# Attention order by a planner: when the sums, the squares, the value transposes and the output weights are given out

## The chip, the cores and the metric

The kernel runs on one core of a Trainium2 chip. The metric is device time in microseconds of one execution. Its engines work side by side: TensorE (PE in the profile, with PEld for its weight loads), VectorE (DVE), ScalarE (ACT), GpSimd (POOL) and SyncE (SP), which issues DMAs.

## The reference

One layer of a decoder trunk on 1024 rows of width 1024. What matters here, cut from the reference:

```python
h = _rmsnorm(x, g_mix);  proj = h @ w_in               # Q, K, V of both groups
# 8 stick-breaking heads of 64, in blocks of 128 queries over the causal prefix
log_survive = lax.cumsum(log_keep, axis=3, reverse=True) - log_keep
weights = jnp.where(strict, jnp.exp(log_beta + log_survive), 0.0)
o_sb = weights @ v                                      # per block
# 4 differential heads: two softmaxes (ALiBi), value width 128
attn = probs[:, :, 0] - lam * probs[:, :, 1];  o_df = attn @ v
o_sb = _rmsnorm(o_sb, g_sb_out);  o_df = _rmsnorm(o_df, g_df_out) * (1.0 - lambda_init)
x = x + jnp.concatenate([o_sb, o_df], axis=-1) @ w_out
# then RMSNorm, a router (1 of 4 groups, 2 of its 4 experts), 16 SwiGLU experts,
# a sigmoid-gated per-layer input and a last RMSNorm
```

The squares of each group's output must be summed over all its heads before a row can be normalised; only then can the output projection of a block of 128 rows begin.

## The kernel before

Float32 operands are split in a high part and a rest (names ending in h or hi, and l or lo), and a product is three matmuls. The stages: input norm and the first pair's projections to about 50 us; the attention, pair by pair, to about 530 us; the output projection in eight blocks of 128 rows (b0 to b7), with the router of the block before; then the experts, the per-layer input and the last norm.

There are 8 pairs of attention work, 0 to 3 stick-breaking and 4 to 7 differential. While a pair's attention runs, TensorE also computes this pair's V (two halves, v0 and v1) and the next pair's K and Q. Pair 7 has no next pair: it carries its own V only, and the weights of the output projection are loaded and split beside it (`out_weights`, L1048 ff: ScalarE writes `woh`, L1061, VectorE the rest `wol`, L1062).

A unit is one head and 256 query rows. Its steps: scores (L361/L362), on VectorE, ScalarE and GpSimd the weights (differential: L432 score and maximum, L439 and L448 exponentials, L450 combination), transposes of the weights (L378, `turn`) with a split to `wth`/`wtl` (L54/L55), value products (L488 to L491) into the one bank `pv`, a copy to `ot` (L499; three buffers), and `finish_o`: the DMA of `ot` to memory, its square on ScalarE (L791) and, for the differential pairs and the last stick-breaking one, the sums over rows as small matmuls with ones (L800) into a score bank.

The order on TensorE is written out by a planner, the class `Mix`, which keeps a model of the time of each engine. It holds five queues: scores S, transposes T, values V, finishes F and projection items P. In each turn `ready_x` says when the head of queue x could go; the first of V, T, S, F that is ready goes, unless the projections lag. `on(eng, ready, dur, first)` models work on another engine; `first` is work emitted under high priority. Only TensorE's order is written by hand (`manual_schedule`); VectorE's and ScalarE's is set by the tile scheduler, with precedence for what stands under `high_priority`. V's projection is drained through `vt` (one buffer, L278 on ScalarE), transposed on TensorE (L283, the `turns` of the diff) and split.

`phase_attention` runs the planner until no projection item is left and at most three finishes are (`len(mix.F) <= 3`); what is left then is mixed with blocks b0, b1 and b2 by `run_items`. A block b of the output projection begins with `normed`: the scale of its rows (`rs_*` on VectorE from `ss`), two kinds of transposes (L1134, L1140), scalings (L1136, L1141), a split, then 16 times three matmuls (L1162 to L1164). `tail` and `routes` of the block before stand among them (L1194, L1210, L1327, L1343).

Of the kernel before, what the change touches and what calls it, by code (L numbers as in the profile page):

```python
# [11 lines left out]
AF = mybir.ActivationFunctionType  # L12
# [231 lines left out]
def evac_k(k, P):  # L244
    nc = k.nc

    def f(s0, s1, ps):
        s = slice(s0, s1)
        for i, (a, b) in enumerate(ROWS2):
            oa, ob = ROWS2[1 - i]  # L250
            nc.scalar.activation(P.K[i][a:b, s], ps[a:b], AF.Copy)
            nc.vector.tensor_tensor(P.K[i][oa:ob, s], ps[a:b], P.K[i][a:b, s].bitcast(FT), OP.subtract)
    return f
# [61 lines left out]
def alloc_pair(k, P, pool):  # L315
    P.K = [pool.tile([128, S], FR, name=f"K{i}") for i in range(2)]
    P.Qh = [pool.tile([128, S], FR, name=f"Qh{i}") for i in range(2)]
    P.Ql = [pool.tile([128, S], FR, name=f"Ql{i}") for i in range(2)]
    P.V = [pool.tile([128, NB, 128], FR, name=f"V{i}") for i in range(2)]


def weights_item(k, P, i, eng=None):
    def f():
        P.W[i] = load_w(k, P.cols[i], eng)
    return (0.0, f)


def value_projection(k, P):

    g = group_items(k, lambda: P.W[2], HALVES, evac_v(k, P))  # L330
    turn = (0.45, lambda: P.turns.pop(0)())
    return g[:4] + [turn], g[4:] + [turn]
# [124 lines left out]
def units_of(k, P):  # L457

    units, OT = [], {}
    for pr in range(NB // 2):  # L460
        for h in range(1 if P.df else 2):
            u = Ctx()
            u.P, u.pr, u.h, u.rows, u.score, u.W = P, pr, h, [], [], {}
            for ii in range(2):
                i = 2 * pr + ii
                u.score.append((i, df_row_items(k, P, i, u.rows) if P.df else sb_row_items(k, P, h, i, u.rows)))
            u.turn = lambda g, u=u: turn_rows(k, u.pr, u.rows, g, u.W)
            u.value = lambda g, u=u: value(k, u, g, OT)
            u.last = P.df or h == 1
            u.finish = lambda u=u: finish_o(k, OT[u.pr], u.P, u.pr)  # L470
            units.append(u)
    return units
# [62 lines left out]
class Mix:  # L535
# [3 lines left out]
    def __init__(self, k, wt):  # L539
        self.k, self.wt = k, wt  # L540
        self.pe, self.at = 0.0, {"act": 0.0, "dve": 0.0, "pool": 0.0}
        self.S, self.T, self.V, self.F, self.P = [], [], [], [], []
        self.zfree, self.tpfree, self.pvfree, self.mmfree = [0.0] * 3, [0.0] * 2, [0.0], [0.0] * 2
        self.done, self.tot = {}, {}
        self.nT = self.nV = 0
        self.emit = lambda c, f: f()

    def on(self, eng, ready, dur, first=False):

        start = max(self.at[eng], ready)  # L550
        self.at[eng] = start + dur
        return (min(start, ready + 0.7) if first else start) + dur

    def add_pair(self, P, p, units, proj):
        main = 0.0
# [65 lines left out]
    def ready_v(self):  # L621
        u, g = self.V[0]
        if g not in u.wready or not u.values(g):
            return None
        return max(u.wready[g], self.pvfree[0] if g == 0 else 0.0)

    def do_v(self):
# [11 lines left out]

    def ready_f(self):  # L640
        u = self.F[0]
        return u.out + 1.0 if u.vals == u.pr + 1 else None

    def do_f(self):
        u = self.F.pop(0)
        self.emit(0.11, u.finish)
        self.on("act", self.pe, 0.4)
        self.pe += 0.3 if u.P.df or u.P.ch == 3 else 0.0

    def ready_p(self):  # L650
        p, kind, c, f, ok = self.P[0]
# [4 lines left out]
    def do_p(self):  # L656
        p, kind, c, f, ok = self.P.pop(0)
        f()
        self.pe += c
        self.done["p", p] += c  # L660
        if kind == "weights":
            self.on("dve", self.on("act", self.pe + 4.0, 1.1), 1.25)
        if kind == "last":
            a = self.on("act", self.pe, 1.2, True)
            self.mmfree = self.mmfree[1:] + [self.on("dve", a, 1.3, True)]
# [25 lines left out]
def run_pairs(k, Ps, qk, n, last):  # L691


    mix = Mix(k, 3)
    us = [units_of(k, P) for P in Ps[:n + 1]]
    every = [u for x in us for u in x]
    state = {"kq": 0, "v": {}}

    def proj(items, p, ok=None, end=None):
        out = []  # L700
        per = NC // 2
        for x, (c, f) in enumerate(items):
            kind = "last" if c > 1 and x % (per + 1 if end is None else per) == per - 1 else "mid"
            out.append([kind, c * 1.05, f, ok if x == 0 else None])
        return out

    for p in range(n + 1):
        P, Q = Ps[p], Ps[min(p + 1, n)]
        v0, v1 = value_projection(k, P)

        def group(items, ok, then):
            out = []
            for x, (c, f) in enumerate(items):
                kind = "first" if x == 0 else "last" if x == 3 else "mid"
                if x == len(items) - 1:
                    g = f
                    f = lambda g=g: (g(), then())
                out.append((kind, c * 1.05, f, ok if x == 0 else None))
            return out

        def counted(p, x):
            return lambda: state["v"].__setitem__((p, x), True)

        def alloc(Q=Q, p=p):
            alloc_pair(k, Q, qk[p % 2])

        def free(p=p):
            return p == 0 or all(u.vals == u.pr + 1 for u in us[p - 1])

        def load(Q, i):  # L730
            return ("weights", 0.0, weights_item(k, Q, i)[1], None)


        w0 = load(Q, 0)
        w1 = load(Q, 1)
        w2 = load(Q, 2)
        turns = [("mid", 0.45, v[4][1], None) for v in (v0, v1)]
        for x in range(2):
            kd, c, f, ok = turns[x]
            turns[x] = (kd, c, lambda f=f, p=p, x=x: (f(), state["v"].__setitem__((p, x), True)), ok)  # L740
        for u in us[p]:
            u.values = lambda g, p=p: (p, g // 2) in state["v"]
        if p == n:
            items = group(v0[:4], None, nothing) + [turns[0]] + [("mid", 0.0, f, None) for f in last[0]]
            items += group(v1[:4], None, nothing) + [turns[1]] + [("mid", 0.0, f, None) for f in last[1]]
            mix.add_pair(P, p, us[p], items)
            break
        K = group_items(k, lambda Q=Q: Q.W[0], HALVES, evac_k(k, Q))
        QQ = group_items(k, lambda Q=Q: Q.W[1], HALVES, evac_q(k, Q, Q.qscale))
        nothing_ = lambda: None  # L750
        kq = ("mid", 0.0, lambda p=p: state.__setitem__("kq", p + 1), None)
        items = [w0] + group(v0[:4], None, nothing_) + [turns[0], w1] + group(v1[:4], None, nothing_)
        items += [("mid", 0.0, alloc, free)]
        g = group(K[:4], None, nothing_)
        items += g[:1] + [turns[1]] + g[1:] + group(K[4:], None, nothing_) + [w2]
        items += group(QQ[:4], None, nothing_) + group(QQ[4:], None, nothing_) + [kq]
        for u in us[p]:
            u.values = lambda g, p=p: (p, g // 2) in state["v"]
        mix.add_pair(P, p, us[p], items)
    for x, u in enumerate(every):  # L760
        before = every[x - 2] if x >= 2 else None
        u.allowed = lambda u=u, before=before: state["kq"] >= u.p and (before is None or before.turns == before.pr + 1)
    return mix
# [18 lines left out]
def finish_o(k, ot, P, pr):  # L782
    nc = k.nc
    q = slice(pr * 256, (pr + 1) * 256)
    nc.sync.dma_start(k.oT_d[P.ch][:, q], ot)
    sums = k.sums[pr // 2][:, pr % 2 * 256:pr % 2 * 256 + 256]
    if P.df or P.ch:
        sq = k.wk.tile([128, 256], FT, name="sq", bufs=2)
    else:
        sq = sums  # L790
    nc.scalar.activation(sq, ot, AF.Square)  # L791
    if not P.df:
        if P.ch:
            nc.gpsimd.tensor_tensor(sums, sums, sq, OP.add)
        if P.ch < 3:
            return
        sq = sums
    ps = bank_z(k, P.df)
    for i in range(2):
        nc.tensor.matmul(ps[:, i:i + 1], sq[:, i * 128:(i + 1) * 128], k.ones, start=True, stop=True)  # L800
    nc.scalar.activation(k.ss[:, 2 * pr:2 * pr + 2, max(P.ch - 3, 0)], ps[:, 0:2], AF.Copy,
                         scale=1.0 if P.df else 0.25)
# [1201 lines left out]
```

## Time and profile before

| what | value |
|---|---|
| median of 3 runs | 1231.78 us (1230.64 to 1232.29) |
| the profiled execution | 1227.81 us |
| its span, first to last instruction | 1226.0 us |
| mean granted clock of TensorE | 0.979 |
| busy PE / DVE / ACT / POOL | 1145.5 / 923.1 / 723.0 / 207.5 us |

The span is the profiled execution less 1.8 us; that execution lies 4.0 us under the median. A window below gives the busy time of each engine in a stretch; a wait is idle time of an engine and what ended it; a timeline gives the start of an instruction, its duration, and in brackets its idle time before.

### The profile page before, as it was taken

The page shows a single profiled execution, that of the slowest core. Times are in us where ns is not written, and L with a number is a line of the kernel's source. Part 1 is how long each engine was busy: PE and PEld are TensorE (multiplying, and loading weights), DVE is VectorE, ACT ScalarE, POOL GpSimd, SP SyncE. Part 2 cuts the span into 40 slices and gives each one's busy share as a digit, 9 for nine tenths or more (in the row PEclk, how much of TensorE's full clock was granted, in tenths as well). Part 3 has the DMA queues.
Part 4 walks back from the last instruction along what each step waited for, and adds up shares of the span by engine and source line. Part 5 has one row for each costly group of instructions (what it writes and reads, how often), then busy time and mean ns, then how long its engine had stood idle before and what let it go on. Part 6 is the DMA issues. An engine that isn't in the chain of part 4 may idle for free. (4 is left out here: it accounts for less than half of the span.)

```text
span 1226.0 us, 22814 instructions
## 1 busy us (share of the span) xinstructions
PE 1145.5 (93%) x8181; PEld 826.5 (67%) x8181; DVE 923.1 (75%) x2144; ACT 723.0 (59%) x1408; POOL 207.5 (17%) x298
## 2 busy tenths in 40 slices
PE   5999999999999999889789899999999999997996
PEld 4766656665666666646444498898998989883443
DVE  7677786766766767769888777777888878765875
ACT  6476766766756576735332365666777767663432
POOL 0133333333200000002331101111112212110000
PEclk9999999999999999879899999999999999999999
DMA  6212021120222121532674878998998999937611
GB/s 208 67 30 74 30 69 32 44 60 27 57 61 65 40 65 53 171 90 102 217 234 148 298 250 262 282 352 265 316 313 283 337 280 325 304 125 298 250 71 52
DMA packets 211756, 202.54 MB, mean 165 GB/s; under 512 B 12697, under 2 KB 182681, under 8 KB 211642
## 3 DMA queue, kind: packets, MB, share of 16 engines
q1 hardware_dynamic: 205688, 180.22, 46.9%
q0 software_dynamic: 5808, 20.58, 4.5%
q8 instruction: 65, 1.06, 0.3%
q14 instruction: 49, 0.40, 0.1%
q10 hardware_dynamic: 146, 0.27, 0.1%
HBM read 163.03 MB, written 29.62 MB: 157 GB/s over the span
## 5 line engine op out<-in xcount | busy, mean ns | idle before, releaser
L228 PE MATMUL mm<-hT,whi 128*128 128x512 f32 (+1 forms) x416 | 210.9, 508 | 2.6 <-DVE rs_v L66 1.4
L229 PE MATMUL mm<-hT,whi 128*128 128x512 bf16 (+1 forms) x416 | 157.0, 377 | 4.1 <-DVE hT L184 4.1
L230 PE MATMUL mm<-hT,wlo 128*128 128x512 bf16 (+1 forms) x416 | 155.7, 374 | 0.0
L1611 PE MATMUL gu<-xh,mhiu 128*128 128x128 f32 (+4 forms) x512 | 155.1, 314 | 0.0
L1611 PE MATMUL gu<-xh,mhig 128*128 128x128 f32 (+4 forms) x512 | 153.9, 308 | 0.0
L1613 PE MATMUL gu<-xbl,mhig 128*128 128x128 bf16 (+4 forms) x512 | 124.6, 243 | 2.6 <-DVE xbl L1524 2.6
L1613 PE MATMUL gu<-xbl,mhiu 128*128 128x128 bf16 (+4 forms) x512 | 124.4, 243 | 0.0
L1614 PE MATMUL gu<-xh,mblg 128*128 128x128 bf16 (+4 forms) x512 | 119.6, 234 | 0.0
L1614 PE MATMUL gu<-xh,mblu 128*128 128x128 bf16 (+4 forms) x512 | 119.3, 233 | 0.0
L55 DVE TENSOR_TENSOR mdl<-mrawd,mdh 128x1024 bf16<-128x1024 f32 x63 | 77.0, 1222 | 44.6 <-ACT mdh L54 39.9
L54 ACT ACTIVATE wth<-tp 128x512 fp32r<-128x512 f32 (+2 forms) x168 | 70.2, 446 | 63.0 <-PE tp L378 41.0
L55 DVE TENSOR_TENSOR wtl<-tp,wth 128x512 fp32r<-128x512 f32 (+2 forms) x168 | 79.2, 493 | 36.7 <-ACT wth L54 35.3
L409 POOL TENSOR_TENSOR row<-row,keep 128x127 f32<-128x127 f32 (+3 forms) x64 | 77.9, 1218 | 143.5 <-DVE keep L408 88.4
L228 PEld LDWEIGHTS mm<-hT,whi 128*128 128x128 f32 x416 | 80.2, 193 | 30.9 <-ACT hT L183 2.0
L55 DVE TENSOR_TENSOR mblg<-mrawg,mhig 128x1024 bf16<-128x1024 f32 x62 | 75.8, 1223 | 29.8 <-ACT mhig L54 29.7
L54 ACT ACTIVATE mdh<-mrawd 128x1024 fp32r<-128x1024 f32 x64 | 67.6, 1056 | 51.8 <-PE ya L1643 47.6
L1611 PEld LDWEIGHTS gu<-xh,mhig 128*128 128x128 f32 x512 | 97.6, 191 | 0.7 <-ACT xh L1523 0.3
L229 PEld LDWEIGHTS <-whi 128*128 128x128 bf16 x416 | 40.7, 98 | 85.0 <-issue 78.6
L1611 PEld LDWEIGHTS gu<-xh,mhiu 128*128 128x128 f32 x512 | 96.7, 189 | 0.0
L408 DVE TENSOR_TENSOR_SCAN keep<-keep,zx 128x128 f32<-128x128 f32 (+3 forms) x64 | 85.4, 1346 | 14.1 <-ACT keep L404 13.4
L46 POOL DMA_INDIRECT y_d<-yo,put x27 | 44.6, 1651 | 290.0 <-ACT yo L1661 185.8
L54 ACT ACTIVATE mhig<-mrawg 128x1024 fp32r<-128x1024 f32 x64 | 67.4, 1053 | 19.2 <-PE gu L1614 11.9
(348 smaller groups left out, 3346.6 us busy)
## 6 DMA issues: line engine op xcount, KB each, us to landing
mrawg<-in_w_expert_gate_dram SPq DMA_DIRECT2D x64, 512.0 KB, 5.8
mrawu<-in_w_expert_up_dram SPq DMA_DIRECT2D x64, 512.0 KB, 6.4
mrawd<-in_w_expert_down_dram SPq DMA_DIRECT2D x64, 512.0 KB, 4.3
wraw<-in_w_in_dram SPq DMA_DIRECT2D x24, 512.0 KB, 3.9
yg<-y_d SPq DMA_DIRECT2D x16, 512.0 KB, 5.7
xt<-in_x_dram SPq DMA_DIRECT2D x8, 512.0 KB, 6.6
oT_d<-ot SPq DMA_DIRECT2D x32, 128.0 KB, 2.1
wraw<-in_w_out_dram SPq DMA_DIRECT2D x8, 512.0 KB, 3.6
```

Of the source, the lines that this page charges most:

```text
L46: i = k.nc.gpsimd.indirect_dma_start(out=out, out_offset=bass.IndirectOffsetOnAxis(ap=idx, axis=0), in_=src, in_offset=None)
L54: nc.scalar.activation(hi, src, AF.Copy)
L55: (eng or nc.vector).tensor_tensor(lo, src, hi.bitcast(FT), OP.subtract)
L228: nc.tensor.matmul(ps, hi[:, c, :], hT[:, c % 4, :], start=(c == 0), stop=False)
L229: nc.tensor.matmul(ps, wv[:, c, :], k.hT[half][2][:, c, o:o + n], start=False, stop=False)
L230: nc.tensor.matmul(ps, lo[:, c, :], hv[:, c % 4, :], start=False, stop=(c == NC - 1))
L408: nc.vector.tensor_tensor_scan(a, a, k.zeros.to_broadcast([128, n]), 1.0, op0=OP.mult, op1=OP.add)
L409: nc.gpsimd.tensor_tensor(beta[:, :n - 1], beta[:, :n - 1], keep[:, 1:n], OP.mult)
L1611: nc.tensor.matmul(ps[:, x], hi[:, c], xh[:, c], start=(c == 0), stop=False)
L1613: nc.tensor.matmul(ps[:, x], hv[:, c], xl[:, c], start=False, stop=False)
L1614: nc.tensor.matmul(ps[:, x], bl[:, c], xv[:, c], start=False, stop=(c == NC - 1))
```

## The change

`Mix.on` models boosted work as starting when it is ready, or at the end of the run that then stands on the engine (before: at most 0.7 us late). A unit's last value item is held back while two of the first three finishes have their values but are not given out. A finish is given out 2.0 us after its output (before 1.0), once a score bank is modelled free, and its sums take that bank. The value transposes of each pair stand two projection items later. The square in `finish_o` gets precedence on ScalarE. The output weights are modelled as work of ScalarE and VectorE, spread among the V items of pair 7, and begin once the values of pair 6 are given out.

```diff
--- before.py
+++ after.py
@@ -539,6 +539,7 @@
     def __init__(self, k, wt):
         self.k, self.wt = k, wt
         self.pe, self.at = 0.0, {"act": 0.0, "dve": 0.0, "pool": 0.0}
+        self.runs = {x: [] for x in self.at}
         self.S, self.T, self.V, self.F, self.P = [], [], [], [], []
         self.zfree, self.tpfree, self.pvfree, self.mmfree = [0.0] * 3, [0.0] * 2, [0.0], [0.0] * 2
         self.done, self.tot = {}, {}
@@ -549,7 +550,10 @@
 
         start = max(self.at[eng], ready)
         self.at[eng] = start + dur
-        return (min(start, ready + 0.7) if first else start) + dur
+        if first:
+            start = max([ready] + [t1 for t0, t1 in self.runs[eng] if t0 <= ready < t1])
+        self.runs[eng] = self.runs[eng][-12:] + [(start, start + dur)]
+        return start + dur
 
     def add_pair(self, P, p, units, proj):
         main = 0.0
@@ -622,6 +626,8 @@
         u, g = self.V[0]
         if g not in u.wready or not u.values(g):
             return None
+        if g == u.pr and sum(x.vals == x.pr + 1 for x in self.F[:3]) > 1:
+            return None
         return max(u.wready[g], self.pvfree[0] if g == 0 else 0.0)
 
     def do_v(self):
@@ -639,13 +645,16 @@
 
     def ready_f(self):
         u = self.F[0]
-        return u.out + 1.0 if u.vals == u.pr + 1 else None
+        if u.vals < u.pr + 1:
+            return None
+        return max(u.out + 2.0, self.zfree[0 if u.P.df else 1])
 
     def do_f(self):
         u = self.F.pop(0)
         self.emit(0.11, u.finish)
-        self.on("act", self.pe, 0.4)
-        self.pe += 0.3 if u.P.df or u.P.ch == 3 else 0.0
+        if u.P.df or u.P.ch == 3:
+            self.pe += 0.3
+            self.zfree = self.zfree[1:] + [self.on("act", self.pe, 0.25)]
 
     def ready_p(self):
         p, kind, c, f, ok = self.P[0]
@@ -660,6 +669,8 @@
         self.done["p", p] += c
         if kind == "weights":
             self.on("dve", self.on("act", self.pe + 4.0, 1.1), 1.25)
+        if kind == "split":
+            self.on("dve", self.on("act", self.pe + 3.0, 1.1), 1.25)
         if kind == "last":
             a = self.on("act", self.pe, 1.2, True)
             self.mmfree = self.mmfree[1:] + [self.on("dve", a, 1.3, True)]
@@ -741,18 +752,21 @@
         for u in us[p]:
             u.values = lambda g, p=p: (p, g // 2) in state["v"]
         if p == n:
-            items = group(v0[:4], None, nothing) + [turns[0]] + [("mid", 0.0, f, None) for f in last[0]]
-            items += group(v1[:4], None, nothing) + [turns[1]] + [("mid", 0.0, f, None) for f in last[1]]
+            done = lambda: all(u.vals == u.pr + 1 for u in us[n - 1])
+            wo = [("split", 0.0, f, done if x == 1 else None) for x, f in enumerate(last[0] + last[1])]
+            g = group(v1[:4], None, nothing)
+            items = group(v0[:4], None, nothing) + wo[:1] + g[:2] + [turns[0]] + g[2:] + wo[1:3] + [turns[1]] + wo[3:]
             mix.add_pair(P, p, us[p], items)
             break
         K = group_items(k, lambda Q=Q: Q.W[0], HALVES, evac_k(k, Q))
         QQ = group_items(k, lambda Q=Q: Q.W[1], HALVES, evac_q(k, Q, Q.qscale))
         nothing_ = lambda: None
         kq = ("mid", 0.0, lambda p=p: state.__setitem__("kq", p + 1), None)
-        items = [w0] + group(v0[:4], None, nothing_) + [turns[0], w1] + group(v1[:4], None, nothing_)
+        g = group(v1[:4], None, nothing_)
+        items = [w0] + group(v0[:4], None, nothing_) + [w1] + g[:2] + [turns[0]] + g[2:]
         items += [("mid", 0.0, alloc, free)]
         g = group(K[:4], None, nothing_)
-        items += g[:1] + [turns[1]] + g[1:] + group(K[4:], None, nothing_) + [w2]
+        items += g[:2] + [turns[1]] + g[2:] + group(K[4:], None, nothing_) + [w2]
         items += group(QQ[:4], None, nothing_) + group(QQ[4:], None, nothing_) + [kq]
         for u in us[p]:
             u.values = lambda g, p=p: (p, g // 2) in state["v"]
@@ -788,7 +802,8 @@
         sq = k.wk.tile([128, 256], FT, name="sq", bufs=2)
     else:
         sq = sums
-    nc.scalar.activation(sq, ot, AF.Square)
+    with k.tc.high_priority(offset=k.boost):
+        nc.scalar.activation(sq, ot, AF.Square)
     if not P.df:
         if P.ch:
             nc.gpsimd.tensor_tensor(sums, sums, sq, OP.add)
```

Lines of the changed kernel from `finish_o` on have numbers 15 above those of before (L800 is now L815, L1162 now L1177).

The first place is TensorE at the V projection of pair 6: `hT_79` is the last row of v0's matmuls, `hT_81` belongs to v1, L283 are v0's transposes. Before:

```order
L229 MATMUL mm<-hT_80,whi 128x512
L230 LDWEIGHTS wlo
L230 MATMUL mm<-hT_79,wlo 128x512
L283 MATMUL mm<-ident,vt 128x128 x4
L228 MATMUL mm<-hT_81,whi 128x512
```

and after the change:

```order
L230 MATMUL mm<-hT_79,wlo 128x512
L228 MATMUL mm<-hT_81,whi 128x512
...
L230 MATMUL mm<-hT_81,wlo 128x512
...
L361 MATMUL z<-K_4596,Qh_4598 128x256
L362 MATMUL z<-K_4596,Ql_4600 128x256
...
L230 MATMUL mm<-hT_81,wlo 128x512
...
L361 MATMUL z<-K_4596,Qh_4598 128x384
L362 MATMUL z<-K_4596,Ql_4600 128x384
L283 MATMUL mm<-ident,vt 128x128 x4
L228 MATMUL mm<-hT_82,whi 128x512
```

The transposes stood right behind v0's last matmul; now four groups of three matmuls of v1 and some scores stand between.

The second place is TensorE where the attention of pair 7 meets the output projection: L1134/L1149 and L1140/L1155 are the first block's scale transposes, L1162/L1177 its first product. Before:

```order
L361 MATMUL zx<-K_5148,Qh_5150 128x384
L362 MATMUL zx<-K_5148,Ql_5152 128x384
L361 MATMUL zx<-K_5148,Qh_5150 128x384
L362 MATMUL zx<-K_5148,Ql_5152 128x384
L1134 MATMUL tp<-ident,rs_y 128x128
L1140 MATMUL tp<-ident,rs_y 128x128 x4
L378 MATMUL tp<-ident,row 128x128 x4
L1134 MATMUL tp<-ident,rs_y 128x128
L488 MATMUL pv<-wth,V_5153 128x256
L1140 MATMUL tp<-ident,rs_y 128x128
L1162 MATMUL mm<-woh_5702,od_5725 128x512
```

and after:

```order
L378 MATMUL tp<-ident,row 128x128 x7
L815 MATMUL z<-ones,sq 128x1 x4
L488 MATMUL pv<-wth,V_5130 128x256
L489 MATMUL pv<-wtl,V_5130 128x256
L491 MATMUL pv<-wth,V_5131 128x256
...
L815 MATMUL zx<-ones,sq 128x1 x2
L1149 MATMUL tp<-ident,rs_y 128x128
L1155 MATMUL tp<-ident,rs_y 128x128 x4
L1149 MATMUL tp<-ident,rs_y 128x128
L1155 MATMUL tp<-ident,rs_y 128x128 x4
L1177 MATMUL mm<-woh_5946,od_5991 128x512
...
L378 MATMUL tp<-ident,row 128x128 x4
```

Before, 13 score items, 9 transposes and 9 value items were left when the hand-written stage ended, and scores of pair 7 stand among the blocks from there on; now no score is left, two transposes and five value items are, and rows of attention alone stand ahead of L1149 (it is row 3264 of TensorE's order, 3198 before).

The third place is ScalarE at a finish in pair 7: L791/L806 is the square, L1061/L1076 the copy of an output weight. Before:

```order
L448 ACTIVATE row<-row,dfr 128x512
L439 ACTIVATE keep,dfm<-keep,dfm 128x512
L1061 ACTIVATE woh_5912<-wraw 128x1024
L1061 ACTIVATE woh_5918<-wraw 128x1024
L791 ACTIVATE sq<-ot 128x256
L801 ACTIVATE ss<-zx 128x2
L439 ACTIVATE row,dfm<-row,dfm 128x640
```

and after:

```order
L499 ACTIVATE ot<-pv 128x256
L816 ACTIVATE ss<-z 128x2
L806 ACTIVATE sq<-ot 128x256
L54 ACTIVATE wth<-tp 128x512
L439 ACTIVATE row,dfm<-row,dfm 128x256
L1076 ACTIVATE woh_6002<-wraw 128x1024
```

The square followed two weight copies; at this finish no weight copy stands between the copy of the output (L499) and its square now, at a later finish of pair 7 one still does.

## Rows read from the trace of the kernel before

**Rows 1.** Windows: busy us of PE, PEld, DVE, ACT, POOL; clock, DMA share, GB/s.

```profile
489.00:531.00 42.00, 32.06 (x158) 22.87 (x156) 33.91 (x119) 29.71 (x62) 1.06 (x6) 0.79 0.49 157
...
531.00:677.50 146.50, 132.59 (x714) 76.53 (x714) 120.14 (x470) 52.08 (x104) 31.29 (x31) 0.95 0.50 164
...
489.00:515.00 26.00, 20.46 (x120) 14.47 (x119) 22.40 (x68) 21.04 (x46) 1.06 (x6) 0.97 0.57 188
...
515.00:527.00 12.00, 8.67 (x29) 6.54 (x29) 8.12 (x41) 6.54 (x14) 0.00 (x0) 0.50 0.47 141
...
560.00:600.00 40.00, 36.34 (x216) 22.86 (x215) 37.15 (x147) 18.79 (x38) 12.75 (x13) 1.00 0.60 204
...
597.00:611.00 14.00, 7.26 (x27) 3.71 (x26) 10.14 (x27) 3.61 (x7) 4.04 (x3) 0.76 0.52 178
```

**Rows 2.** Waits of PE, 50 to 489 us: total, times, longest.

```profile
PE pv L489 <- DVE wtl L55: 7.6, 8, 1.4
...
PE mm L283 <- ACT vt L278: 3.5, 6, 0.7
...
PE tp L378 <- DVE wtl L55: 2.8, 1, 2.8
...
PE z L800 <- DVE dfm L432: 2.1, 2, 1.1
```

**Rows 3.** Timeline of PE around pair 7 and the first block (start, us).

```profile
489.03 0.28 PE L361 MATMUL z<-K,Qh 128*128 128x256 f32 x1
...
513.84 1.01 PE L800 MATMUL zx<-ones,sq 128*128 128x1 f32 x4 [4.87 <-ACT sq L791]
...
530.94 0.80 PE L1162 MATMUL mm<-woh,od 128*128 128x512 f32 x1
```

**Rows 4.** Timeline of ACT ahead of the wait at 513.84.

```profile
511.49 2.00 ACT L1061 ACTIVATE woh<-wraw 128x1024 fp32r<-128x1024 f32 x2
...
513.38 0.41 ACT L791 ACTIVATE sq<-ot 128x256 f32<-128x256 f32 x1
```

**Rows 5.** Lines of DVE by form, 489 to 531 us.

```profile
L1062 DVE TENSOR_TENSOR wol<-wraw,woh 128x1024 bf16<-128x1024 f32 x7 | 8.4, 1218 | 0.2 <-ACT woh L1061 0.2
...
L432 DVE CUSTOM_DVE_ANT_0 keep<-z,dist 128x384 f32<-128x384 f32 x3 | 1.7, 556 | 1.0 <-PE z L362 0.9
...
L55 DVE TENSOR_TENSOR wtl<-tp,wth 128x512 fp32r<-128x512 f32 x4 | 2.7, 686 | 0.1
```

**Rows 6.** Timeline of DVE: scales and scalings of the first output blocks.

```profile
522.10 0.17 DVE L66 TENSOR_SCALAR rs_v<-ss 128x10 f32<-128x10 f32 x1
...
526.28 0.17 DVE L100 SCALAR_TENSOR_TENSOR rs_y<-rs_i,rs_y 128x10 f32<-128x10 f32 x1
...
527.02 1.12 DVE L1136 SCALAR_TENSOR_TENSOR od<-od,gn,tp 128x128 f32<-128x128 f32 x4 [0.57 <-PE tp L1134]
...
528.06 0.74 DVE L1141 SCALAR_TENSOR_TENSOR od<-od,gn,tp 128x512 f32<-128x512 f32 x1
```

**Rows 7.** Timeline of ACT: the splits behind them.

```profile
529.34 0.60 ACT L54 ACTIVATE wth<-tp 128x512 fp32r<-128x512 f32 x1 [1.76 <-PE tp L378]
...
529.84 1.05 ACT L54 ACTIVATE od<-od 128x1024 fp32r<-128x1024 f32 x1
```

**Rows 8.** Waits of PE, 495 to 680 us.

```profile
PE dsm L1210 <- DVE od L55: 6.7, 1, 6.7
...
PE dsm L1327 <- DVE A L1325: 4.4, 3, 2.1
...
PE dsm L1343 <- DVE row L1336: 1.3, 1, 1.3
```

**Rows 9.** Timeline of PE: blocks 3 and 7 of the output projection.

```profile
609.36 0.60 PE L1162 MATMUL mm<-woh,od 128*128 128x512 f32 x1
...
610.06 0.60 PE L1162 MATMUL mm<-woh,od 128*128 128x512 f32 x1
...
677.10 0.39 PE L1164 MATMUL mm<-woh,od 128*128 128x512 bf16 x1
```

## Prediction

> **What bounds the kernel now.** The page first: TensorE is busy 1145.5 of 1226.0 us, and its chain of waits ends in the last norm and says nothing of the middle. So I read the page's slices, then TensorE's waits by stage, then the seam between attention and output projection in the timeline. From the experts on (about 700 us) nothing that the change touches is left; there it is worth nothing. What counts is when block b7 of the output projection ends, 677.4 us [rows 9].
>
> Up to pair 7's first score at 489.0 us [rows 3] TensorE waits in short pieces: eight times for a split of weights before a value product, 7.6 us in all; six times for the V copy before the value transposes, 3.5; once 2.8 for a split before transposes; twice for a score bank at the sums L800, 2.1 [rows 2].
>
> The seam from 489 to 531 us is worse. TensorE is busy 32.06 of 42 us at a granted clock of 0.79 [rows 1]. At 513.84 its sums waited 4.87 us for the square of an output [rows 3], which on ScalarE stood behind two weight copies of 2.00 us [rows 4]. After that idle stretch the clock stood at 0.50, the lower of its two levels, 1.2 against 2.4 GHz (515 to 527 us: 8.67 of 12 us busy at that level) [rows 1]. Behind it, in the blocks, TensorE waits 6.7 us for a split before the router's product and 5.7 us in the routing steps [rows 8], with a clock of 0.76 around the first [rows 1].
>
> **How I price an order.** I give each row of TensorE's order the mean time from its start to the next start in the trace, waits and the half-clock stretch left out. As an example three matmuls of a block take 610.06 - 609.36 = 0.70 us [rows 9], so 128 threes are 89 us. By these slots both orders hold 155 us from pair 7's first score to the end of b7. Before, 25.1 of them lie ahead of the first block's first matmul (489.03 to 530.94: 41.9 us elapsed) and 129.9 behind (530.94 to 677.4: 146.5 elapsed) [rows 3, 9]. So 16.8 us are lost ahead of it and 16.6 behind. After the change 2.1 us more of work lie ahead of pair 7's first score, 35.3 between it and the first block, and 117.6 behind. The term to forecast is what is lost in each stretch.
>
> **Ahead of pair 7.** The value transposes stand two projection items behind the V copy, four threes of matmuls of about 0.7 us each, 2.7 us; the waits were at most 0.7 [rows 2]. All 3.5 us go, hidden by v1's matmuls and, for v1's transposes, by K's. Of the bank waits (2.1) I take 1.6, since a finish now asks for a free bank. The model of boosted work now lets a split wait out the run in front of it, so value items come later where it is a long one: half of 7.6, 3.8, and half of the 2.8, 1.4. Against that, by the slots, twelve stick-breaking value items now stand only 1.8 to 2.0 us behind their transposes, where none stood closer than 2.3. If a quarter wait as long as the eight do today (0.95 each), that is 2.9 back. Sum 3.5 + 1.6 + 3.8 + 1.4 - 2.9 = 7.4 us gained. Bounds: 0.6 (the transposes alone, less the new waits) and 13 (all four rows of [rows 2], 16.0, less the new waits). Pair 7 then begins at 489.0 - 7.4 + 2.1 = 483.7.
>
> **The seam.** The wait for the square goes: at that finish the weight copies no longer stand between, and the sums come 2 us later. But its price of 4.87 us and the half clock behind it are not simply saved, because what filled TensorE there has moved too. With 13 score items no longer left for the blocks, the 35.3 us of work ahead of the first block are V's projection (6.8) and pair 7's attention alone. That stretch is VectorE's: from pair 7's first score maximum (L432) to its last combination (L450) its order holds 24 score passes with their reads (14.7 us), 18 splits of weights and V (8.1), nine combinations (7.4), six remainders of output weights (6.8) and small steps (6.1), 43.1 us in all at slots of which the commonest are 0.56 to 1.22 us [rows 5]. VectorE is busy 0.86 of 489 to 515 us and 0.93 of 560 to 600 [rows 1]; at 0.88 the stretch lasts 49 us (bounds 46 to 50).
>
> Then a chain follows beside which nothing is left: the last combination's transposes 0.4, the split 0.6 on ScalarE and twice 0.69 on VectorE [rows 5, 7], two interleaved sets of row scales, the single one 4.2 us among other work [rows 6], I take 2.9 for both at their own durations, a transpose 0.3, scalings 1.12 + 0.74 [rows 6], the split on ScalarE 1.05 [rows 7], and about 1.2 us of handing over between engines: 9.7 us. The first block starts at 483.7 + 49 + 9.7 = 542.4, against 530.9 now. It is later by 11.5 us, with 12.3 us less to do behind it.
>
> Behind it the routing waits stay, as `tail` and `routes` are unchanged. The 6.7 us wait came in a stretch where VectorE was 0.93 busy [rows 1]; with pair 7's score passes gone from there I take a quarter of it and its half clock off, 14 lost instead of 16.6. Bounds: 6.5 (both gone) and 20. The end of b7 comes at 542.4 + 117.6 + 14 = 674.0, against 677.4.
>
> So the change gives 3.4 us. The profiled execution goes from 1227.8 to 1224.4; against the median of the runs, which lies 4.0 above that execution, I predict 1228.5.
>
> What carries work on SyncE's and GpSimd's queues: the weight loads of the output projection are issued with their splits, so they come spread among V's items and not in two blocks; DMA share there is 0.57 [rows 1], and I take nothing for it. The DMA of an output leaves 1 us later with its finish; its reader is the first block, later by 11 us, so it is hidden.
>
> **A rule against the change.** The row on the half clock (8.67 of 12 us busy, clock 0.50) shows that TensorE did not return to full speed while it worked in short pieces between waits for VectorE [rows 1]. The Trainium skill, "TensorE: Matmul & The Clock Gate", section "A second HAM failure mode: psum-queue depth-cycling", says that frequent small idle gaps between groups of matmuls can make the clock swing between its two levels, and that throughput suffers from it. The trace agrees as far as that row goes; no run yet shows pair 7 without filler. By that rule the second rival below, 1238.7, would be the forecast; by the rows of the stretches that begin busy, which show a clock of 0.97 and more, it is not.
>
> **The rivals.**
> First, nothing measurable: the waits ahead of pair 7 give 4.0 instead of 7.4 us, because value products wait for splits that run late anyway. All else equal the end comes at 677.4, 1231.8. For it: 10.4 of the 16.0 us are waits for splits, which the change doesn't make any shorter. Against: 3.5 us for the V copy are certain.
>
> Second, slower: in the stretch of pair 7 alone TensorE falls to 1.2 GHz and stays there. It decides once its work at half speed outlasts VectorE's 43 us. The 35.3 less V's 6.8 are 28.5 us at full speed, 57 at half; with 6.8 ahead and some 5 of the chain in which it does nothing, 69 us from pair 7's start to the first block, not 58.7. That is 10 us more, 6.9 over now: 1238.7. For it: the work of 513 to 531 is the same kind, and stood at half clock. Against: that stretch began with 4.87 us of nothing, and in the new order the gaps should be shorter than a microsecond or two each.
>
> Third, a larger gain: without pair 7's score passes beside the blocks VectorE is in time for the router's product, and the 6.7 us wait and its half clock go as a whole: 14 becomes 6.5, the end 666.5, the time 1221. For it: VectorE's busy 0.93 before that wait. Against: what it waited for, the split od L55 [rows 8], belongs to the blocks, whose order is hardly changed.
>
> That the planner's edits don't do what they say I hold for unlikely, since the orders show each of them; the sums in the stretch of pair 7 alone still come behind a weight copy at one finish, which would cost its 1 us.
>
> **How the numbers follow.** The forecast 0.40 (its own range 1225 to 1231.5), nothing measurable 0.20, the half clock 0.30, the larger gain 0.10. About 0.2%, 2.5 us, is what a measurement of this kernel can tell from no change. Of the forecast 0.33 lies under 1229.3, 0.05 within, and 0.02 over; with the larger gain that makes faster 0.43. Same is 0.20 of the first rival less 0.03 that falls slower, and the 0.05: 0.22. Slower is 0.30 + 0.03 + 0.02 = 0.35. The range reaches from 1218, past the larger gain with the upper bound of the waits, to 1240, past the half clock.
>
> **What would show it.** Waits of TensorE for `vt` at L283: none. Waits before 489 us for splits: about half of 7.6. Pair 7's first score at 484 (482 to 490). The square's wait of 4.87 gone. From there to L1177, 58 us with VectorE busy 0.85 or more and the clock at 1.0; a clock near 0.5 over tens of microseconds there is the second rival. L1177 at 542, b7's end at 674. I am wrong on the mechanism if the stretch to L1177 is much shorter than 58 us, or if the end of b7 moves by something behind L1177 alone.

## The result and the profile after

The changed kernel takes 1246.88 us (1246.22 to 1248.66, 4 runs) against 1231.21 of the kernel before: a ratio of 1.0138, 95% interval 1.0125 to 1.0152. It is slower; forecast was 1228.5. The profiled execution took 1246.22 us. One of the five executions of e9 below took 1843.81 us at a granted clock of 0.558 and is left out of that run's figures; e13 is the same kernel again, for its trace.

Windows of the changed kernel, columns as in [rows 1]: two stretches of the attention, then from pair 7 to the first block, and from there to the end of b7.

```profile
50.00:121.00 71.00, 66.05 (x370) 42.63 (x376) 49.44 (x65) 44.85 (x100) 21.72 (x27) 0.98 0.23 54
383.40:444.00 60.60, 56.09 (x334) 41.57 (x336) 40.13 (x135) 39.42 (x91) 2.47 (x15) 0.97 0.14 40
498.40:559.80 61.40, 47.25 (x249) 39.79 (x247) 46.57 (x171) 39.79 (x89) 2.15 (x12) 0.78 0.28 92
559.80:694.40 134.60, 120.59 (x614) 64.55 (x626) 109.02 (x413) 40.67 (x80) 29.33 (x27) 0.95 0.53 177
```

TensorE's timeline of the changed kernel, which answers to [rows 3, 9]: pair 7's first score, the first block's first product, the last product of b7.

```profile
498.39 0.36 PE L361 MATMUL zx<-K,Qh 128*128 128x256 f32 x1
...
559.79 0.79 PE L1177 MATMUL mm<-woh,od 128*128 128x512 f32 x1
...
694.03 0.39 PE L1179 MATMUL mm<-woh,od 128*128 128x512 bf16 x1
```

Pair 7 begins at 498.4 (483.7 forecast, 489.0 before), the first block 61.4 us later (58.7 forecast, 41.9 before), and b7 ends 134.6 us after that, at 694.4 (131.6 forecast, 146.5 before). Most of the miss is ahead of pair 7, 14.7 us; the other stretches are off by 2.7 and 3.0. Against the kernel before, 9.4 us were lost ahead of pair 7 and 7.5 from there to b7's end.

TensorE's waits of the changed kernel from 50 to 498 us, the answer to [rows 2]:

```profile
PE pv L489 <- DVE wtl L55: 10.9, 13, 1.9
PE tp L378 <- DVE dfr L442: 1.7, 1, 1.7
PE tp L378 <- DVE wtl L55: 1.7, 4, 0.5
PE tp L378 <- DVE row L450: 1.1, 1, 1.1
```

The waits for `vt` are gone and the bank waits of 2.1 nearly (0.3 left), but value products wait longer for their split. All waits together are 17.6 us, against 16.8 before: no gain. And from 498 to 560 us:

```profile
PE tp L378 <- DVE row L450: 5.2, 3, 1.9
PE z L361 <- DVE dfm L432: 4.4, 4, 2.1
PE tp L378 <- DVE dfm L437: 1.8, 1, 1.8
```

Two of the 9.4 us by which pair 7 is late arose ahead of the attention. The same instruction, near the start of the attention, in the kernel before and then in the changed one:

```profile
52.94 0.47 PE L228 MATMUL mm<-hT,whi 128*128 128x512 f32 x1 [0.58 <-DVE K L252]
```

```profile
54.90 0.47 PE L228 MATMUL mm<-hT,whi 128*128 128x512 f32 x1 [0.58 <-DVE K L252]
```

Another 2.1 us, by the prediction's slots, are work that the new order puts ahead of pair 7. Some 5 us are left that it lost, where 7.4 were to be gained. Counted from the attention's first score, pair 7 begins at 437.2 us before and at 444.6 now.

### The profile page after: what moved, and what is told of

Same layout as the page of the kernel before. It is cut to its first block, busy times and chain, and to the rows that moved or that the text cites. A ratio compares the mean times of both kernels' runs of the same rounds, so it can differ in the third digit from the quotient of the medians.

```text
span 1244.5 us, 22698 instructions
## 1 busy us (share of the span) xinstructions
PE 1155.1 (93%) x8075; PEld 837.6 (67%) x8181; DVE 927.2 (75%) x2144; ACT 724.3 (58%) x1408; POOL 206.0 (17%) x298
## 5 line engine op out<-in xcount | busy, mean ns | idle before, releaser
L228 PE MATMUL mm<-hT,whi 128*128 128x512 f32 (+1 forms) x416 | 212.7, 512 | 2.6 <-DVE rs_v L66 1.5
L229 PE MATMUL mm<-hT,whi 128*128 128x512 bf16 (+1 forms) x377 | 143.2, 380 | 4.1 <-DVE hT L184 4.1
L228 PEld LDWEIGHTS mm<-hT,whi 128*128 128x128 f32 x416 | 81.3, 195 | 31.1 <-ACT hT L183 2.0
L488 PE MATMUL pv<-wth,V 128*128 128x256 f32 x240 | 78.5, 346 | 1.0 <-DVE ot L504 0.6
```

Source lines behind the costliest of these rows:

```text
L228: nc.tensor.matmul(ps, hi[:, c, :], hT[:, c % 4, :], start=(c == 0), stop=False)
L229: nc.tensor.matmul(ps, wv[:, c, :], k.hT[half][2][:, c, o:o + n], start=False, stop=False)
L488: nc.tensor.matmul(po, v0, wh, start=first, stop=False)
```

## The experiments

Each group of runs had the kernel before beside it: 1230.30 us with e1 to e4, 1229.32 with e5 to e8, 1230.24 with e9 to e12, 1229.76 with e13 to e16. The ratios are to those runs.

The planner's own record of its choices (its model's clock, not the chip's) gave the first theory. A finish now needs a free score bank, and scores stand ahead of finishes in the choice (`now[0]` over "vtsf"), so each bank that comes free goes to a score. In the planner's clock finishes came 2.1 to 5.8 us after the unit's last value before, and 3.1 to 53.5 us after the change. The unit behind may then not give its last value; the next K waits for all values of the pair before (`free`); and at the end pair 7's first finish comes only when no score is left.

**Where the bank rule acts.** Four runs of the changed kernel.

```diff
 e1  return u.out + 2.0
 e2  return max(u.out + 2.0, self.zfree[..] if u.p == 7 else 0.0)
 e3  return max(u.out + 2.0, self.zfree[..] if u.p <= 5 else 0.0)
 e4  ready_f and do_f as before the change
```

> The changed kernel; a finish no longer asks for a free score bank (it still comes 2.0 us after its output). First theory: scores stand ahead of finishes in the planner's choice and take each bank that comes free, so finishes wait for many scores; that holds back the next units' last values and the next K, and at the end the first finish of pair 7, so that nothing is left beside the blocks. Then both losses go: first block's first product near 533 us, 1226 to 1232. Rival, the model of boosted work gives value products out too early and the weights' order delays the seam: the time stays at 1240 to 1247.

Measured: 1236.02 us (ratio to before 1.0046, 1.0028 to 1.0064). The rule costs 10.9 us of the changed kernel's time, more than the rival allows, but 5.7 above the kernel before remain: half a hit. The first block's first product comes at 536.3, pair 7's first score still at 498.75: what came back lies behind pair 7's start, nothing ahead of it.

> The changed kernel, the bank asked for by the finishes of pair 7 alone. First theory: what is lost ahead of pair 7 (7 us by the traces, of them 2 before the attention) goes, the loss at the seam (10) stays: 1238 to 1242, pair 7's first score at 484 to 491. Rival, the loss ahead comes from the model of boosted work: 1245 to 1248.

Measured: 1249.05 (1.0161). Pair 7's first score at 497.1, so the loss ahead of it did not go, and e1 has it too: the theory misses, this loss has another cause. The seam is late, 56.8 us from pair 7 to the first block, as it says.

> The changed kernel, the bank asked for by the finishes of pairs 0 to 5 alone. First theory: the loss ahead of pair 7 stays, the seam is as before with scores left for the blocks: 1234 to 1238. Rival, the seam is late because of the weights' new order: 1244 to 1248.

Measured: 1246.66 (1.0146). The seam itself is short again, 37.6 us (498.5 to 536.1), but the blocks behind it took until 693.6; the expected 10 us were lost there, with routing waits of 6.7 and 5.1 us. From pair 7's start to b7's end TensorE also stood 13.7 us longer at the granted clock of 0.50 than in e1 (44.4 against 30.7). Neither foresaw that.

> The changed kernel with the finish's rule and cost as before (1.0 us after its output, no bank). First theory: within 3 us of the run without the bank alone, 1225 to 1232; if the 2.0 us that I forecast as a gain at the sums are worth something, it is slower than that run by up to 2 us. Rival as for the first run: 1240 to 1247.

Measured: 1239.38 (1.0078): 7 us over the theory's range, just under the rival's, and 3.4 above e1 where 2 to 3 were allowed. What is sure from e1 and e4: without the bank the seam has its filler back and the kernel is still slower than before.

**The model of boosted work and the moved transposes.** e5 is the kernel before with the new `on`; e6 the changed kernel with the old one; e7 as e6 and without the bank; e8 the kernel before with the moved transposes.

```diff
 e5, undone in e6 and e7
-        return (min(start, ready + 0.7) if first else start) + dur
+        if first: start = max([ready] + [t1 for t0, t1 in self.runs[eng] if t0 <= ready < t1])
 e8
-        ... + [turns[0], w1] + group(v1[:4], ..)      items += g[:1] + [turns[1]] + g[1:]
+        ... + [w1] + g[:2] + [turns[0]] + g[2:]       items += g[:2] + [turns[1]] + g[2:]
```

> The kernel before with the new model of boosted work alone. Theory: the model now holds a split for started as soon as it is ready, so value products are given out before the split has landed: waits of value products for wtl rise from 7.6 to about 17 us ahead of 489 us, as in the run without the bank, and the time to 1237 to 1242. Rival, those waits come from the moved value transposes: waits stay near 7.6, time 1229 to 1233.

Measured: 1242.82 (1.0114, 1.0098 to 1.0131), just above the range. TensorE's waits of this run from 50 to 498 us:

```profile
PE pv L489 <- DVE wtl L55: 13.5, 12, 2.1
PE mm L283 <- ACT vt L278: 1.9, 3, 1.0
```

13.5 us against 7.6 [rows 2], at once and alone: the opposite of the 3.8 that I had forecast as a gain from this edit.

> The changed kernel with the model of boosted work as before, the bank kept. Theory: ahead of pair 7 it loses only what the late finishes cost, about 5 us less than the changed kernel; the seam stays late (no score left): 1238 to 1243. Rival, the two faults are one (the late finishes made the room for early value products): 1245 to 1249.

Measured: 1244.10 (1.0125): 2.8 better than the changed kernel, above the expected range and below the rival's. Its waits of value products for `wtl` are 6.1 us against 10.9 in the changed kernel, but 7.2 us of waits for `row` stand in their place (1.1 there). In full company the model of boosted work costs far less than alone.

> The changed kernel with the model of boosted work as before and no bank asked for by a finish. What is left of the change: finishes 2.0 us after their output, the held-back last value, the value transposes two items later, the square's precedence, the output weights' place. Theory: the waits for vt (3.5), the bank waits (2.3) and part of the 4.87 us at the square are gained and nothing lost: 1222 to 1229. Rival, the time went in the weights' new place or the moved transposes: 1233 to 1240.

Measured: 1235.69 (1.0074): the rival. Its seam is short (33.4 us, VectorE 29.07 busy), so what is lost is ahead of it: pair 7 begins 444.1 us after the first score, 6.9 later than before, and value products wait 13.6 us for `wtl` and 2.3 for V.

> The kernel before with the value transposes two projection items later, alone. Theory as forecast: the six waits for vt, 3.5 us, go and nothing comes in their place: 1226 to 1229. Rival: an order so dense gives the wait back at the splits of values: 1230 to 1234.

Measured: 1234.83 (1.0034, 1.0018 to 1.0049): the rival's upper end and a little over; the seven runs lie between 1230.69 and 1235.38. Its waits from 50 to 489 us:

```profile
PE pv L489 <- DVE wtl L55: 10.9, 10, 2.1
PE tp L378 <- DVE wtl L55: 2.8, 1, 2.8
PE pv L488 <- DVE V L55: 2.3, 2, 1.1
PE z L801 <- POOL sums L795: 1.4, 1, 1.4
```

The 3.5 us for `vt` went; value products now wait 2.3 for V itself, which its later transposes deliver later, and 3.3 more for their splits.

**Single parts, and the parts that pay.** e9 and e13 are the kernel before with the rule for finishes and the held-back value alone; e10 with the output weights' place and the square's precedence alone; e11 adds the moved transposes in the differential pairs only (`if P.df:` around the lines of e8); e12 adds `u.out + (2.0 if u.P.df else 1.0)`, no bank.

> The kernel before with the finish's rule alone: 2.0 us after its output, a free score bank asked for, the last value of the next unit held back. Theory: the finishes starve behind the scores, no score is left for the output blocks, the first block's first product comes near 550 us (530.9 before): 1238 to 1244. Rival, the seam was late because of the weights' new place and the early value products: 1229 to 1233.

Measured: 1241.70 (1238.31 to 1243.17, four runs; 1.0100, 1.0083 to 1.0117): the theory's time.

> The kernel before with the finish's rule alone, once more for its trace. Theory: most of its 12 us are lost between pair 7's first score and the first block (61 us as in the changed kernel, 42 before); ahead of pair 7 it loses less than 4 us. Rival: it loses ahead of pair 7, where late finishes hold back values, and the seam only shifts.

Measured: 1244.45 (1.0118). Pair 7 begins at 497.4 and the first block at 549.2: 51.8 us, not 61. It loses ahead of pair 7 as well, more than the theory allows. One place is pair 5's start. There are the matmuls of line L228 (the first of each three of a projection) from 391 to 401 us, columns PE busy, PEld busy, clock, DMA share and GB/s, and under them all of the engines as in [rows 1], in the kernel before, then in e13:

```profile
391.00:401.00 10.00, 4.63 (x9) 1.71 (x9) 1.00 0.22 68
391.00:401.00 10.00, 10.00 (x61) 6.83 (x60) 6.84 (x29) 7.38 (x22) 0.35 (x2) 1.00 0.22 68
```

```profile
391.00:401.00 10.00, 0.00 (x0) 0.00 (x0) 0.93 0.01 1
391.00:401.00 10.00, 6.54 (x36) 5.20 (x35) 7.97 (x38) 8.02 (x21) 0.39 (x2) 0.93 0.01 1
```

The changed kernel has no such matmul there either and is busy 6.54 us too. In the planner's clock no projection item goes for 28.6 us there (8.6 before), because pair 4's last value comes at 327.1 instead of 311.4 and the next K waits for it. Without filler TensorE in the changed kernel waits 1.7 us for `dfr` and 1.1 for `row` (listed above), and the clock falls, 0.97 over 383 to 444 us.

> The kernel before with the output weights' new place and the square's precedence alone; the order up to pair 7 is that of before. Theory: the 4.87 us wait for the square and part of its half clock go, as in the run with both faults undone (seam shorter by 4): 1224 to 1228. Rival, the weights now run late into the first block and take it back: 1229 to 1232.

Measured: 1227.83 (0.9981, 0.9972 to 0.9991), 2.4 under before: the theory, at its upper end. In the seam the sums wait 2.3 us for squares in two places, not 4.9, and the first block comes 39.1 us after pair 7's start (41.9 before). The run does not tell the two parts apart.

> As the run before, and the value transposes two items later in the differential pairs alone, where the trace of the transposes alone lost 0.8 us less than nothing between 330 and 470 us of work and the kernel before 3.7. Theory: 4 us under the run of weights and square: 1220 to 1225. Rival, the gain there was made up of waits that the late stick-breaking pairs had left: same as that run.

Measured: 1215.63 (0.9893, 0.9876 to 0.9909), 12.2 under e10, three times what I expected. Windows of e11 from pair 7's first score to the first block, and on to b7's end:

```profile
484.20:518.90 34.70, 30.02 (x157) 21.06 (x157) 31.78 (x117) 28.62 (x62) 1.05 (x6) 0.90 0.59 190
518.90:663.50 144.60, 129.31 (x698) 74.61 (x712) 121.20 (x471) 53.09 (x105) 30.13 (x31) 0.98 0.51 168
```

and its waits from 50 to 484 us:

```profile
PE pv L489 <- DVE wtl L55: 7.6, 8, 1.4
PE tp L378 <- DVE wtl L55: 2.8, 1, 2.8
PE mm L283 <- ACT vt L278: 1.8, 3, 0.7
```

The `vt` waits of the differential pairs and the bank waits are gone with nothing in their place, and the seam is 34.7 us against 41.9 [rows 1], at a clock of 0.90. By the two traces, 14.6 us apart, 7.0 lie ahead of pair 7 (430.3 us after the first score, 437.3 in e10) and 6.6 from there to b7's end, where TensorE stood 13.7 us at the granted clock of 0.50 against 23.9 in e10. The expectation had priced the waits alone. This is the version that beats both kernels.

> As the run before, and the sums of the differential pairs 2.0 us after their output. Theory: the bank waits at the sums (2.3 us) go too: 1218 to 1224, 1 to 2 us under it. Rival: the sums were hidden, no difference within 1 us.

Measured: 1216.92 (0.9903): the rival, or nearly: 1.3 us apart, with intervals that overlap. The theory had nothing to gain, since the bank waits no longer stand in e11's list.

**Tests of the two causes in the stick-breaking pairs.** e14 is e8 with `if not P.df:`; e15 is e5 with 0.7 us added to each boosted start; e16 is e11 with `ready + 1.4` for `ready + 0.7`.

> The kernel before with the value transposes two items later in the stick-breaking pairs alone. Theory: the V wait there goes, but value products now wait for V's split and for wtl: 1236 to 1240, slower than with all pairs (1234.8). Rival, each small edit of the order moves the time by some us either way and the place does not matter: 1229 to 1234.

Measured: 1237.74 (1.0062, 1.0044 to 1.0080): the theory. The same move costs 8.0 us here and pays in the differential pairs. Its waits from 50 to 499 us, in full down to 1 us:

```profile
PE pv L489 <- DVE wtl L55: 10.9, 10, 2.1
PE tp L378 <- DVE wtl L55: 2.8, 1, 2.8
PE pv L488 <- DVE V L55: 2.3, 2, 1.2
PE z L805 <- DVE dfm L432: 1.5, 2, 1.1
PE z L805 <- POOL sums L799: 1.4, 1, 1.4
PE mm L283 <- ACT vt L278: 1.0, 2, 0.7
```

2.5 us of waits for `vt` went; 2.3 for V and 3.3 for `wtl` came.

> The kernel before with the new model of boosted work, which here adds 0.7 us to every boosted start. Theory: value products no longer go too early, waits for wtl ahead of 489 us fall from 13.5 to under 8 us, time from 1242.8 to 1229 to 1234. Rival, the loss of that model has another cause (where it places the rest): 1238 to 1244.

Measured: 1230.37 (1.0005, 0.9993 to 1.0018): the theory. Waits of value products for `wtl` are

```profile
PE pv L489 <- DVE wtl L55: 2.0, 2, 1.4
```

down from 13.5, and all 12.5 us are back; transposes now wait 5.9 for `row` instead. (The 0.7 us stand on every boosted start here, so this is later than the old model and not the old model again.)

> The fastest order (weights' place, square's precedence, transposes in the differential pairs) with the old model's bound of 0.7 us raised to 1.4. Theory: the eight waits for wtl, 7.6 us, shrink to half: 1210 to 1214. Rival: later value products hold up transposes and finishes and the order of the seam changes: 1216 to 1225.

Measured: 1225.64 (0.9976, 0.9961 to 0.9990): the rival. Its value waits fell to 4.5 us, yet it is 10 us slower than e11. Pair 7 begins 430.2 us after the first score, as in e11; the loss lies behind it, 188.2 us to b7's end against 179.4, of which the waits are 25.1 against 18.9.

## Why the prediction was wrong, step by step

**The step that failed** is "Ahead of pair 7": "Sum 3.5 + 1.6 + 3.8 + 1.4 - 2.9 = 7.4 us gained". The runs showed some 5 us lost there. This table, from one trace each, has the time from the attention's first score to pair 7's, TensorE's waits in it, its time at the granted clock of 0.50, and the time from pair 7's first score to b7's end:

| run | to pair 7 | waits | at 0.50 | pair 7 to b7's end |
|---|---|---|---|---|
| before | 437.2 | 16.8 | 3.4 | 188.5 |
| changed kernel | 444.6 | 17.6 | 10.2 | 196.0 |
| e1, without the bank | 445.3 | 21.7 | 10.2 | 187.0 |
| e4, finish's rule as before | 451.0 | 23.3 | 13.7 | 184.6 |
| e6, old model | 445.8 | 16.1 | 13.7 | 192.4 |
| e7, both undone | 444.1 | 20.1 | 10.2 | 186.3 |
| e13, finish's rule and held-back value alone | 444.3 | 15.2 | 13.7 | 193.6 |
| e5, model alone | 447.1 | 21.3 | 13.7 | 189.4 |
| e8, transposes in all pairs alone | 441.5 | 18.9 | 10.2 | 188.6 |
| e14, transposes in stick-breaking pairs alone | 445.5 | 21.6 | 10.2 | 187.6 |
| e10, weights' place and square alone | 437.3 | 17.5 | 3.4 | 186.0 |
| e11, as e10, transposes in differential pairs | 430.3 | 13.2 | 0.0 | 179.4 |

Term by term:

- The transposes, 3.5: the waits went as said. "Hidden by v1's matmuls" was true and not enough: I counted who waits for `vt` and not who waits for V. In the stick-breaking pairs that is the value products; there the move costs (e14: 8.0 us), in the differential pairs it pays (e11 against e10). In e7, where it still stands, the waits for V and the late pair 7 are there too.
- The bank waits, 1.6 of 2.1: nearly gone in the changed kernel. But the price of asking for a bank was set at nothing. The finish's rule with the held-back value costs 11.5 to 14.7 us alone (e9, e13), 7.1 of them ahead of pair 7. Within the change the bank is worth 10.9 (e1), but behind pair 7's start: 187.0 us to b7's end without it, 196.0 with it.
- "The model of boosted work now lets a split wait out the run in front of it, so value items come later": wrong in sign. As the code reads, where no recorded run covers the moment the new model has no delay at all, and value products go before their split has landed. e5 has 13.5 us of those waits, and e15, with 0.7 us added to each start, has 2.0 and the time of before. The term of 3.8 was a loss of 5.9 in e5. In the changed kernel these waits rose by 3.3, and with the old model they are 6.1 (e6), but time came back little. The 2.9 for new waits was too small beside the 5.9 as well. Of the 1.4 at the transposes 1.1 came (2.8 to 1.7), and 2.8 us of waits for `dfr` and `row` beside it.
- The clock had no term. After waits TensorE stood at half speed near 99, 300 and 400 us; the stretch near 300 is in the kernel before too, the other two are new. In the seam of the changed kernel value products follow each other every 0.21 us at a clock of 0.50 (552 to 554 us) and every 0.12 at full speed (545 to 547 us); so, as an estimate, at most half of the time at 0.50 is lost. In e14 the added waits (4.8) and half of the added time at 0.50 (3.4) make 8.2 of the 8.3 us by which pair 7 is later, in e5 4.5 and 5.2 make 9.7 of 9.9. In the changed kernel 0.8 and 3.4 make 4.2 of the some 5. Not every run closes so well: in e13 it is 3.6 of 7.1, part of which is work moved ahead of pair 7, and in e8 5.5, more than the 4.3 lost.

**The seam** held in kind and nearly in size: no filler, 61.4 us against 58.7, and 134.6 behind against 131.6. In part that was luck. To the end of the last combination it took 50.8 us, 49 forecast:

```profile
498.40:549.20 50.80, 38.13 (x207) 31.79 (x205) 39.61 (x133) 36.72 (x82) 1.79 (x10) 0.83 0.34 111
547.87 1.28 DVE L450 SCALAR_TENSOR_TENSOR row<-keep,dfr,row 128x1024 f32<-128x1024 f32 x1
```

VectorE was busy 39.61 us there and not 43.1, and 0.78 of the stretch and not 0.88: two errors that nearly cancel. TensorE and VectorE waited for each other in turn, as the waits for `row` and `dfm` above show. The chain behind took 10.6 us, 9.7 forecast. The clock of 0.78 instead of 1.0 is the second rival in part; its 69 us were too many, since TensorE came back to full speed between. The Trainium skill, "TensorE: Matmul & The Clock Gate", section "A second HAM failure mode: psum-queue depth-cycling", lets frequent short idle gaps make the clock swing; the trace agrees in so far as the clock stood at 0.50 from 519 to 529, 536 to 543 and 550 to 563 us and at full speed between. That filler keeps the clock up is not shown: the kernel before had filler in its seam and 0.79 [rows 1], e11 had it and 0.90.

**The square**: its wait is gone in the changed kernel. Its precedence and the weights' place together are worth 2.4 us by themselves (e10), where 2.3 us of waits for squares are left.

**The range** ended at 1240 because I let new waits cost 2.9 us at most ahead of pair 7 and put the slower case in the seam alone. The case that came, both at once, had no place in it.

**What stays open.** Alone the finish's rule with the held-back value costs 11.5 to 14.7 us, the model of boosted work 13.5, the transposes 4 to 5.5, sum about 31; together with the parts that pay they cost 16. Each is enough to make pair 7 some 4 to 10 us late, and with the bank or the model or both undone it is as late as before the undoing (table). e6 and e1 show the overlap: the model is worth up to 2.8 us with the bank, and without it nothing that can be told (e1 against e7, 0.3 us). The changed kernel with the transposes of the stick-breaking pairs put back was not run, nor the held-back value or the 2.0 us of the finishes by themselves; so how the loss ahead of pair 7 divides within the change is not shown. Why the parts overlap, and which order in the blocks costs e3 and e16 their time, the runs do not settle.

## What to carry to other kernels

Before counting a moved step's wait as gained, list who waits for its result, in each kind of stage that it is moved in: the same two-item move cost 8 us in one kind and belonged to the fastest version in the other. Where a planner sets the order, a new condition on an item that stands last in its choice can starve it (finishes up to 53.5 us late here); look at what it holds back, by the planner's own record, before pricing what it saves. And the parts of a change are worth timing apart: of this one three parts, one of them in half of the pairs, are 1.1% faster than before, the whole 1.4% slower.

## What the runs showed of the hardware

In the kernel before and the changed one the same instruction stands at 52.94 and at 54.90 us (shown above). Over the 17 traces of this case the attention's first score begins between 51.8 us (before) and 54.2 us (e6), though the 260 rows of TensorE ahead of it are the same in all. So about 2 us of a difference between two single traces need no cause in the order of the work, and stages are better compared from a common first instruction.
